# Four heads in lockstep, and TensorE's order written out, in the recurrent part of a diffusion block

## The chip, the core and the metric

The kernel runs on one core of a Trainium2 chip. The metric is the device time of one execution in microseconds; the median of two runs is given for the kernel before. The engines are named as in the profile: PE (TensorE, with PEld for its weight loads), DVE (VectorE), ACT (ScalarE), POOL (GpSimd) and SP, whose queue issues nearly all DMA transfers.

## What is computed

One layer on 512 latent tokens of 1,024 channels, with 256 context tokens ahead of them. A normed and modulated h is multiplied by w_in; the columns feed a Hyena branch, a two-way RWKV-7 branch and 2,048 gates. Both branches are projected, merged under the gates and projected again; a mixture of 16 experts (2,048 wide, 64 tokens each) follows, whose weights are 403 MB. The recurrence is, for each of 8 heads of 64 channels and each direction:

```python
def step(S, inp):
    w_t, k_t, v_t, a_t, b_t = inp[:5]
    sa = einsum('bhij,bhj->bhi', S, a_t)
    S = S * w_t + sa[..., None] * b_t + v_t[..., None] * k_t
    y = einsum('bhij,bhj->bhi', S, inp[5])
    return S, y
# y = groupnorm(y forward + y backward) + bonus, times a gate from a low-rank projection
# gates: sigmoid(h @ w_in[:, gate columns]);  mixed = (g_hy * y_hy + g_rw * (y_rw @ rw_proj)) @ w_out
```

The state starts from a scan over the context. All values are float32.

## The kernel before

The program has stages: modulation, norms and the filter; the Hyena part, which also makes the columns of the recurrent part; the recurrent part; merge, output projection and router; the experts.

The recurrent part is worked in chunks of 64 tokens (`C`), eight of the sequence and four of the context each way. Two heads make a group `g`, since two heads of 64 channels fill the 128 partitions; there are four groups, and each has three batches `bt` of four chunks in both directions. For a batch, `pieces` makes the scaled keys, rates and receptances (`pus` matmuls, a scan on DVE, exponentials on ACT); `scores` makes the masked 64x64 scores `M` of a chunk and writes them to the DRAM tile `N_d`; `inverses` reads them back as 16x16 blocks (`nb`), inverts these on DVE and writes them to `X_d`; `levels` reads those (`XX`) and builds the 64x64 inverses with 32x32 matmuls; `values` transposes values (`pv`) and keys (`pb`). Then `steps` runs the four chunks one after another: `p1` (values and state against scores and keys), a copy to `X1` on DVE, `p2` (the inverse), copies to `UV` on DVE and ACT, `p3` (the new state) and the outputs into the bank `ya`. `epilogue` norms and gates a group's output and stores it to `y_d`.

Work of one group is ahead of or behind that of the next by the strings `ORD0` and `ORD1` and by scheduler priorities (`HP`, `HPB`); the scheduler orders all engines. `gates(i)`, sixteen tiles of 128 gate columns at the end of the program, is what the scheduler puts into TensorE's free time. Each takes a 512 KB tile of w_in from a pool of `NRAW` = 3 buffers and multiplies it by `hraw`, the h that stays in SBUF. `pump` adds matmuls of zeros (`zl`) behind each of `p1`, `p2` and `p3`, and `plv` two behind each step of `levels`:

```python
for _ in range(n):            # pump: into the idle half of the bank bk
    mm(bk[...], zl, zw, start=True, stop=True)
# plv: for i in range(NPL): mm(half, zl, zeros) -- ahead of each level's products
pump(NP1, p1, last)           # steps, behind p1; NP2 behind p2, NP3 behind p3
```

A float32 matmul of at most 512 columns is two records in the trace, so a count of records is twice that of the matmuls. All DMA transfers of the part are issued by SP in the order of its queue; where one has to wait for a buffer, those behind it wait too. After the stage, `halves` (line 1235) loads projection weights through the same raw buffers.

## Time and profile before

| | |
|---|---|
| runs | 1875.36 and 1876.31 us, median 1875.84 |
| profiled execution | span 1886.6 us, the only time given for it |
| recurrent stage | 322 to 782 us |
| merge, output projection, router | 782 to 928 us |
| experts | 928 us to the end |
| busy over the span | PE 90%, PEld 59%, DVE 36%, ACT 23%, POOL 11% |

A row of the table of windows has start and end of a stretch, its length, the busy time of PE, PEld, DVE, ACT and POOL (instructions in brackets), TensorE's granted clock as a share of 2.4 GHz, the mean busy share of the 16 DMA engines and the GB/s they moved. A group by line has line, engine, operation, tiles written and read, shapes and count, then busy time and mean ns of one, then the idle time of the engine just ahead of it and what ended it. The timeline has start and length in us. Tile numbers are left out of the names there.

### The profile page before, as it was taken

How to read it: one execution, taken by the hardware profiler on the slowest of the kernel's cores; microseconds unless marked ns; L12 is line 12 of the kernel's file. 1: busy time of each engine (PE TensorE's matmuls, PEld its weight loads, DVE VectorE, ACT ScalarE, POOL GpSimd, SP SyncE). 2: the span in 40 equal slices, each digit the busy share in tenths (PEclk: the TensorE clock that was granted, in tenths of full speed). 3: DMA queues.
4: the chain of work that ended last, by engine and by line, in shares of the span. 5: the costliest groups of instructions: out<-in, count | busy, mean ns of one | idle time of the engine just before them, and what ended most of it. 6: DMA issues, size and time to landing. Idle time of an engine off the chain costs nothing.

```text
span 1886.6 us, 32798 instructions
## 1 busy us (share of the span) xinstructions
PE 1702.4 (90%) x14006; PEld 1107.5 (59%) x14006; DVE 681.9 (36%) x1520; ACT 434.5 (23%) x941; POOL 214.5 (11%) x255
## 2 busy tenths in 40 slices
PE   8898999999999999789599999889899898998985
PEld 3466786667666767668475545555455454554542
DVE  4765875867584742363500202002020020200203
ACT  3544531434453433333100000000000000000001
POOL 0534102422131300020000000000000000000000
PEclk5799999899999899999699999999999999999998
DMA  7255543433222221571799999999999999999995
GB/s 304 95 187 192 172 159 114 144 83 67 64 69 40 57 47 41 179 269 62 295 402 427 426 427 427 426 427 426 427 427 427 426 427 426 426 426 427 426 427 231
DMA packets 143292, 516.46 MB, mean 274 GB/s; under 512 B 83259, under 2 KB 87499, under 8 KB 118572
## 3 DMA queue, kind: packets, MB, share of 16 engines
q1 hardware_dynamic: 139824, 509.68, 68.8%
q10 hardware_dynamic: 3324, 4.70, 0.7%
q8 instruction: 110, 1.80, 0.4%
q14 instruction: 34, 0.28, 0.0%
HBM read 490.98 MB, written 23.36 MB: 273 GB/s over the span
## 4 chain that ended last, share of the span: by engine, by line
PE 39%; DMA 14%; DVE 3%; ACT 1%; issue 1%; POOL 0%; SPq 0%; DVEq 0%; ACTq 0%; POOLq 0%
PE ph L1425 17%; DMA exp_w<-in_exp_w 12%; PE py L1438 10%; PE px L1392 3%; PE pso L1460 3%; PE pht L249 1%; DVE hd L216 1%; PE po L1245 1%; PE po L1242 1%; PE po L1243 1%; ACT hT L212 1%; PE pl L1326 0%; PE pbq L1406 0%; PE pbp L1402 0%; DMA w_hy_proj<-in_hy_proj 0%
## 5 line engine op out<-in xcount | busy, mean ns | idle before, releaser
L1425 PE MATMUL ph<-exp_w,xe 128*64 128x256 f32 x4096 | 469.2, 380 | 26.7 <-DMA exp_w<-in_exp_w 26.7
L1425 PEld LDWEIGHTS ph<-exp_w,xe 128*64 128x64 f32 x4096 | 318.2, 137 | 194.8 <-issue 63.4
L216 DVE TENSOR_TENSOR hd<-ph,hd 128x256 f32<-128x256 f32 x64 | 27.2, 425 | 674.5 <-PE ph L1425 674.5
L1438 PE MATMUL py<-exp_w,hT 128*64 128x512 f32 x1024 | 236.8, 598 | 24.8 <-ACT hT L212 24.8
L1438 PEld LDWEIGHTS py<-exp_w,hT 128*64 128x64 f32 x1024 | 78.4, 136 | 138.7 <-issue 92.8
L719 PE MATMUL pgate<-hraw,w_gate 128*128 128x256 f32 x512 | 148.0, 409 | 0.7 <-ACT yo L212 0.3
L213 ACT ACTIVATE hd<-ph 128x256 f32<-128x256 f32 x64 | 24.5, 383 | 431.7 <-PE ph L1425 431.7
L719 PEld LDWEIGHTS pgate<-hraw,w_gate 128*128 128x128 f32 x512 | 90.6, 198 | 19.2 <-issue 3.8
L212 ACT ACTIVATE hT<-pht 128x256 f32<-128x256 f32 x64 | 24.5, 383 | 284.6 <-PE pht L249 284.6
L1392 PEld LDWEIGHTS px<-OH,xn 128*128 128x128 f32 x512 | 65.8, 197 | 23.4 <-issue 22.4
L1399 POOL COPY sel<-kcon 16x128 f32<-16x128 f32 x8 | 2.2, 283 | 609.4 <-PE pbq L1406 609.4
L1460 PE MATMUL pso<-ye,oT 128*128 128x512 f32 x128 | 68.7, 628 | 0.7 <-ACT ye L212 0.7
L1392 PE MATMUL px<-OH,xn 128*128 128x128 f32 x512 | 68.0, 282 | 0.9 <-DVE OH L223 0.9
L249 PE MATMUL pht<-kcon,hd 128*128 128x128 f32 x128 | 28.0, 301 | 36.1 <-DVE hd L216 35.9
L216 DVE TENSOR_TENSOR mo<-pso,mo 128x512 f32<-128x512 f32 x56 | 38.4, 691 | 39.3 <-PE pso L1460 39.3
L249 PEld LDWEIGHTS pht<-kcon,hd 128*128 128x128 f32 x128 | 12.9, 141 | 65.2 <-DVE hd L216 65.2
L882 PE MATMUL ps<-ar,bk 64*64 64x64 f32 (+1 forms) x512 | 46.5, 277 | 3.6 <-POOL bk L216 2.0
L882 PEld LDWEIGHTS ps<-ar,bk 64*64 64x64 f32 (+1 forms) x512 | 37.4, 177 | 16.5 <-POOL bk L216 5.0
L1443 DVE COPY ye<-py 64x512 f32<-64x512 f32 x16 | 11.1, 694 | 95.8 <-ACT ye L212 95.8
L216 POOL TENSOR_TENSOR mw<-mw 128x256 f32<-128x256 f32 x32 | 31.5, 1001 | 99.2 <-DVE mw L219 99.2
L288 PE MATMUL p<-zl 128*128 128x256 bf16 x140 | 40.0, 286 | 0.0
L212 ACT ACTIVATE sf<-st,fs 128x64 f32<-128x64 f32 x80 | 24.3, 341 | 49.6 <-DVE st L219 49.4
(396 smaller groups left out, 2549.7 us busy)
## 6 DMA issues: line engine op xcount, KB each, us to landing
exp_w<-in_exp_w SPq DMA_DIRECT2D x192, 2048.0 KB, 31.0
mw<-in_mod_w SPq DMA_DIRECT2D x48, 512.0 KB, 3.9
w_gate<-in_w_in SPq DMA_DIRECT2D x16, 512.0 KB, 4.9
w_h<-in_w_in SPq DMA_DIRECT2D x12, 512.0 KB, 4.1
w_c<-in_w_in SPq DMA_DIRECT2D x12, 512.0 KB, 5.6
g_d<-gt SPq DMA_DIRECT2D x16, 256.0 KB, 4.7
gg<-g_d SPq DMA_DIRECT2D x16, 256.0 KB, 5.5
w_o<-in_w_out SPq DMA_DIRECT2D x8, 512.0 KB, 5.3
```

The costliest lines, as they stand in the source:

```text
L212: return A.activation(out, in_, func, scale=scale, **kw)
L213: return A.activation(out, in_, func, bias=bias, scale=scale, **kw)
L216: e.tensor_tensor(out, a, b, op=op)
L249: TE.transpose(out, in_, ident[0:n, 0:n])
L288: mm(bk[:, 256:256 + NPW].rearrange("p (a b) -> p a b", b=P), zl, zw, start=True, stop=True)
L719: mm(pt[:, n:n + 256], w[:, k, :], hraw[:, k, n:n + 256], start=k == 0, stop=k == KD - 1)
L882: mm(pss[h][r, j * W:(j + 1) * W], BK[d](c)[HR[h], r], AR[d](c)[HR[h], 0:W], start=True, stop=True)
L1242: mm(pt, lhs[0][a], rhs[0][b], start=i == 0, stop=False)
L1392: mm(pt[:, k4 * P:(k4 + 1) * P], xn[:, n, k * P:(k + 1) * P], OH[:, n].rearrange("p a b -> p (a b)"), start=n == 0, stop=n == 3)
L1425: mm(ph[i][64 * hf:64 * hf + 64, 0:256], xe[:, k, 64 * e1:64 * e1 + 64], ws[i][:, k, hf * 256:(hf + 1) * 256], start=k == 0, stop=k == KD - 1)
L1438: mm(py[64 * dh:64 * dh + 64, :], hT_[:, i * P + 64 * hf:i * P + 64 * hf + 64], w2[:, 2 * hf + i, dh * 512:(dh + 1) * 512], start=b == 0 a ...
L1460: mm(pt, oT[:, n * P:(n + 1) * P], ye[:, dh * 512:(dh + 1) * 512], start=True, stop=True)
```

## The change

The recurrent part is written anew. Four heads (two groups, `sg`) go in lockstep, so that there are six units of one batch of two groups, and each matmul block, copy and state update covers four heads. TensorE's order in the stage is written out by `weave`, which runs through the units, the epilogues and the gates as streams with assumed times (`GRP`, `HOP`) and takes the first that is free; the other engines and queues are still ordered by the scheduler. There are no matmuls of zeros in the stage. The scores are made in quarters, 64 rows by 64 columns, and for the chunks of the sequence in two parts. Values are transposed once in the Hyena part, written to `vt_d`, and read back by 48 loads. h is written to `h_d` and read back in four quarters of 128 tokens (`hh`, one buffer); the gates are made for a quarter at a time, so that each 512 KB weight tile is loaded four times: 64 loads, through raw buffers of which there are now two. The decay weights of all groups are loaded at the start through one buffer. Keys (`BK`) have one buffer.

**TensorE, a chunk of the recurrence** (line numbers of the kernel at hand; the numbers in tile names are the program's; `p` is p1, p2 or p3, `zl` the zeros). Before, late in the last group:

```order
L1070 MATMUL p_7802<-st_7793,ar_6564 64x64 x2
L1070 MATMUL p_7802<-st_7797,ar_6601 64x64 x2
L288 LDWEIGHTS zl
L288 MATMUL p_7802<-zl 128x256
L719 MATMUL pgate_8188<-hraw,w_gate_8186 128x256 x2
L1076 MATMUL p_7813<-X_7801,xf_2382 64x64 x4
L288 LDWEIGHTS zl
L288 MATMUL p_7813<-zl 128x256
L719 MATMUL pgate_8188<-hraw,w_gate_8186 128x256
L1085 MATMUL p_7821<-UV_7500,BT_7502 64x64
```

Now, in the fourth unit:

```order
L1044 MATMUL p_6019<-st_5997,AR_4499 64x64 x8
L688 MATMUL pgate_6040<-hh_5428,w_gate_6041 128x128 x8
L1050 MATMUL p_6051<-X_6018,xf_2442 64x64 x8
L688 MATMUL pgate_6040<-hh_5428,w_gate_6062 128x128 x8
L1058 MATMUL p_6072<-UV_5407,BT_5408 64x64 x8
...
L1075 MATMUL yb_6084<-AR_4499,st_5997 64x64 x8
```

Each block has eight matmuls in place of four (rows that repeat for p1's first half and the outputs are left out between the last two), the zeros are gone, and a whole gate tile, eight 128-column matmuls, stands in a hop.

**SP, around the first inverses.** Before, in the first group of the stage:

```order
L715 DMA w_gate_7966<-in_w_in 128x1024
L889 DMA N_d_2372<-M_2460 64x8x64
L889 DMA N_d_2372<-M_2461 64x8x64
L903 DMA nb_2504<-N_d_2372 64x16x16
L715 DMA w_gate_7988<-in_w_in 128x1024
...
L715 DMA w_gate_8010<-in_w_in 128x1024
L930 DMA X_d_2374<-rb_2505 64x16x16
L931 DMA X_d_2374<-rt_2506 64x16x16
...
L964 DMA X_2722<-X_d_2374 32x16x32 x4
```

Now, in the first unit (`hh` is h read back, `N_d`, `nb`, `X_d` and `X` the way of scores and inverses through DRAM):

```order
L686 DMA w_gate_2891<-in_w_in 128x1024
L891 DMA nb_2804<-N_d_2433 128x16x16
L1158 DMA hh_2888<-h_d 128x1024
L693 DMA g_d<-gt_2885 128x4x128
L686 DMA w_gate_2907<-in_w_in 128x1024
L686 DMA w_gate_2932<-in_w_in 128x1024
L918 DMA X_d_2435<-rb_2805 128x16x16
L919 DMA X_d_2435<-rt_2806 128x16x16
L686 DMA w_gate_2942<-in_w_in 128x1024
L939 DMA X_3032<-X_d_2435 32x16x32
L686 DMA w_gate_2963<-in_w_in 128x1024
L939 DMA X_3032<-X_d_2435 32x16x32
```

Gate weights stand between all legs of the inverses' way; 23 of their loads are ahead of the last loads of `X`, where six were.

**TensorE, the end of the stage.** Before:

```order
L1097 MATMUL ya_7547<-ar_6601,st_7839 64x64 x2
L719 MATMUL pgate_8210<-hraw,w_gate_8208 128x256 x2
L1120 MATMUL pmu_7873<-y_7871,kcon 128x512
L719 MATMUL pgate_8210<-hraw,w_gate_8208 128x256 x4
L1127 MATMUL pva_7878<-kcon,sq_7876 128x2 x4
L719 MATMUL pgate_8210<-hraw,w_gate_8208 128x256 x6
L1136 MATMUL pvb_7888<-kcon,vw_7886 128x128 x4
L1141 MATMUL pg_7896<-sg,gup_5994 128x512
L719 MATMUL pgate_8232<-hraw,w_gate_8230 128x256 x16
```

Now:

```order
L1044 MATMUL p_7852<-st_7830,AR_6513 64x64 x8
L1050 MATMUL p_7870<-X_7851,xf_2442 64x64 x8
...
L1075 MATMUL yb_7881<-AR_6513,st_7830 64x64 x8
L1096 MATMUL pmu_7901<-Y_2474,kcon 128x512
L1104 MATMUL pva_7906<-kcon,sq_7904 128x2 x4
L1114 MATMUL pvb_7916<-kcon,vw_7914 128x128 x4
L1120 MATMUL pg_7924<-sg,gup_7899 128x512
L1096 MATMUL pmu_7930<-Y_2474,kcon 128x512
L1104 MATMUL pva_7935<-kcon,sq_7933 128x2 x4
L1114 MATMUL pvb_7945<-kcon,vw_7943 128x128 x4
L1120 MATMUL pg_7953<-sg,gup_7928 128x512
L1215 MATMUL ppr_8029<-yh_7991,wh_hy_proj 128x512
```

The gates no longer lie beside the last epilogue; they end 426 rows ahead of it, and two epilogues follow one another.

The core of the diff:

```diff
-HP = 2000
-HPB = 300
-ORD0 = 'P0ail1b^2ucxjvw'
-ORD1 = "P0aiXuy'l12x^bcjY^ZvwE"
-NP1, NP2, NP3, NPW = 1, 1, 1, 256
...
-NRAW = 3
+NRAW = 2
...
+GRP, HOP = 0.65, 1.45
+NMS, NAR, NBK, NUV, NBT = (3, 2), 3, 1, 2, 2
...
-                ts(V, hraw[:, k, :], ph, modA[:, 0, k, 0:1], mcol[:, 0, k, 0:1], ALU.mult, ALU.add)
-                tt((V, G)[HB[k]], hT[1][:, k, :], hraw[:, k, :], hT[0][:, k, :], ALU.subtract)
+                hraw = ep.tile([P, T], F32, tag="hraw", bufs=3, name=f"hraw{k}")
+                ts(V, hraw, ph, modA[:, 0, k, 0:1], mcol[:, 0, k, 0:1], ALU.mult, ALU.add)
+                tt((V, G)[HB[k]], hT[1][:, k, :], hraw, hT[0][:, k, :], ALU.subtract)
+                SY.dma_start(out=h_d[:, :, k].rearrange("h p t -> p h t"), in_=hraw.rearrange("p (h t) -> p h t", h=4))
...
+                        vt = hp.tile([P, 6, P], F32, tag="vt", name=f"vt{m}")
+                        for a, b in ((0, 4), (4, 6)):
+                            pv = pxx(f"pv{m}{a}")
+                            for i in range(a, b):
+                                transpose(pv[:, (i - a) * P:(i - a + 1) * P], cz[:, i * P:(i + 1) * P])
+                            act(vt[:, a:b].rearrange("p n c -> p (n c)"), pv[:, 0:(b - a) * P], AF.Copy)
+                        SY.dma_start(out=vt_d[m - 8].rearrange("(n p) c -> p n c", p=P), in_=vt)
...
-        def gates(i):
-            o = HY + RW + (i % 2) * D + (i // 2) * P
-            w = filler[0](f"w_gate{i}").rearrange("p (k f) -> p k f", k=KD)
-            SY.dma_start(out=w, in_=w_in[o // P])
-            pt = pfl(f"pgate{i}")
-            for n in (0, 256):
+        def gates(i, q, h):
+            pt = pfl(f"pgate{q}{i}")
+            for n in range(4):
+                o = HY + RW + ((i + n) % 2) * D + ((i + n) // 2) * P
+                w = raw_tile(f"w_gate{q}{i + n}").rearrange("p (k f) -> p k f", k=KD)
+                SY.dma_start(out=w, in_=w_in[o // P])
                 for k in range(KD):
-                    mm(pt[:, n:n + 256], w[:, k, :], hraw[:, k, n:n + 256], start=k == 0, stop=k == KD - 1)
-            t_ = fp.tile([P, T], F32, tag="stg", bufs=NST, name=f"gt{i}")
+                    mm(pt[:, P * n:P * n + P], w[:, k, :], h[:, k, :], start=k == 0, stop=k == KD - 1)
+                    if k % 4 == 3:
+                        yield 0.9, 0.0
+            t_ = fp.tile([P, T], F32, tag="stg", bufs=NST, name=f"gt{q}{i}")
             act(t_, pt, AF.Tanh, scale=0.5)
-            SY.dma_start(out=g_d[i], in_=t_)
+            SY.dma_start(out=g_d[i:i + 4, :, q * P:q * P + P].rearrange("n p t -> p n t"),
+                         in_=t_.rearrange("p (n t) -> p n t", n=4))
...
+            def weave(streams):
+                at, wait, todo = [0.0] * len(streams), [None] * len(streams), list(range(len(streams)))
+                while todo:
+                    free = [i for i in todo if wait[i] is None or wait[i]()]
+                    i = next((i for i in free if at[i] <= clock[0]), None)
+                    if i is None:
+                        clock[0] = min(at[i] for i in free)
+                        continue
+                    wait[i] = None
+                    r = next(streams[i], False)
+                    if r is False:
+                        todo.remove(i)
+                    elif callable(r):
+                        wait[i] = r
+                    else:
+                        clock[0] += r[0]
+                        at[i] = clock[0] + r[1]
...
+                        for j in range(4):
+                            o = C * (4 * d + j)
+                            for r in HR:
+                                for h in range(2):
+                                    bk = BK[HR[h], gi, d, at(d, j)].rearrange("p a t -> p (a t)")
+                                    mm(pss[h][r, o:o + C], bk[:, r], AR[HR[h], gi, d, at(d, j), cols_], start=True, stop=True)
...
                     p1 = bank("st", 2, f"p1{nm}{j}")
-                    for d in range(2):
-                        c = cs[d][j]
-                        o = d * C
-                        for h in range(2):
-                            last = mm(p1[HR[h], o:o + C], M[h][:, d, j, 0:C], uv[:, d, ju, 64 * h:64 * h + 64], start=d == 0,
-                                      stop=first and d == 1)
+                    for gi, d, h in quad:
+                        mm(four(p1)[HR[h], gi, d], M[h][:, gi, d, j], UV[:, gi, d, j, 64 * h:64 * h + 64],
+                           start=gi == 0 and d == 0, stop=first and gi == 1 and d == 1)
+                    yield GRP, max(0.0, t_st - clock[0] - GRP)
                     if not first:
-                        for d in range(2):
-                            c = cs[d][j]
-                            o = d * C
-                            for h in range(2):
-                                last = mm(p1[HR[h], o:o + C], AR[d](c)[HR[h], 0:C], st[d][HR[h]], start=False, stop=d == 1)
-                    pump(NP1, p1, last)
-                    V.tensor_copy(X1.rearrange("p d i -> p (d i)"), p1[:, 0:2 * C])
+                        for gi, d, h in quad:
+                            mm(four(p1)[HR[h], gi, d], AR[HR[h], gi, d, lc[d], 0:C], st[HR[h], gi, d], start=False,
+                               stop=gi == 1 and d == 1)
+                    V.tensor_copy(X1, four(p1))
+                    yield GRP, HOP
                     p2 = bank("st", 2, f"p2{nm}{j}")
-                    for d in range(2):
-                        for h in range(2):
-                            last = mm(p2[HR[h], d * C:(d + 1) * C], X[d][HR[h], j], X1[HR[h], d], start=True, stop=True)
-                    pump(NP2, p2, last)
-                    p23 = p2[:, 0:2 * C].rearrange("p (d i) -> p d i", d=2)
-                    V.tensor_copy(uv[0:64, :, ju, 0:64], p23[0:64])
-                    act(uv[64:128, :, ju, 64:128], p23[64:128], AF.Copy)
-                    if n < NCH - 1:
+                    for gi, d, h in quad:
+                        mm(four(p2)[HR[h], gi, d], X[HR[h], gi, d, j], X1[HR[h], gi, d], start=True, stop=True)
+                    V.tensor_copy(UV[0:64, :, :, j, 0:64], four(p2)[0:64])
+                    act(UV[64:128, :, :, j, 64:128], four(p2)[64:128], AF.Copy)
+                    yield GRP, HOP
+                    old = st
+                    if bt < 2 or j < 3:
                         p3 = bank("st", 2, f"p3{nm}{j}")
-                        for d in range(2):
-                            for h in range(2):
-                                last = mm(p3[HR[h], d * C:(d + 1) * C], btt[:, d, jh, 64 * h:64 * h + 64],
-                                          uv[:, d, ju, 64 * h:64 * h + 64], start=True, stop=True)
-                        pump(NP3, p3, last)
+                        for gi, d, h in quad:
+                            mm(four(p3)[HR[h], gi, d], BT[:, gi, d, j, 64 * h:64 * h + 64], UV[:, gi, d, j, 64 * h:64 * h + 64],
+                               start=True, stop=True)
+                        st = new_state(j)
+                        if first:
+                            tt(V, flat4(st), flat4(four(p3)), by4(F[:, j]), ALU.mult)
+                        else:
+                            tt(V, st, four(p3), old, ALU.add)
+                            tt(V, flat4(st), flat4(st), by4(F[:, j]), ALU.mult)
+                        t_st = clock[0] + GRP + HOP + 0.4
+                        yield GRP, 0.0
                     if bt:
...
-            run(ORD0, (0, False))
-            for g in range(4):
-                pair[0], pair[1] = pair[1], None
-                run(ORD1, (g + 1, g == 3))
-            for i in range(16):
-                gates(i)
+            units = [dict(sg=n % 2, bt=n // 2, nm=f"{n % 2}{n // 2}", N_d=N_d[n % 2], X_d=X_d[n % 2], xf=xfs[n % 2]) for n in range(6)]
+            def unit(n):
+                u = units[n]
+                yield lambda: n < 3 or n - 3 in done
+                yield lambda: n < 1 or n - 1 in filled
+                yield from pieces(u)
+                yield 0.0, 10.0
+                yield from scores(u, 0)
+                inverses(u)
+                t_inv = clock[0] + 22.0
+                yield lambda: n < 2 or n - 2 in done
+                if u["bt"]:
+                    yield from scores(u, 1)
+                yield from values(u)
+                filled.add(n)
+                yield lambda: n < 1 or n - 1 in levelled
+                yield 0.0, max(0.0, t_inv - clock[0])
+                yield from levels(u)
+                levelled.add(n)
+                yield from steps(u)
+                done.add(n)
+            def endings(sg):
+                yield lambda: 4 + sg in done
+                for g in (2 * sg, 2 * sg + 1):
+                    yield from epilogue(g)
+            def all_gates():
+                for q in range(4):
+                    hh = fp.tile([P, KD, T // 4], F32, tag="hh", name=f"hh{q}")
+                    SY.dma_start(out=hh, in_=h_d[q])
+                    for i in range(0, 16, 4):
+                        yield from gates(i, q, hh)
+            with tc.manual_schedule(engines={mybir.EngineType.PE}):
+                weave([unit(n) for n in range(6)] + [endings(0), endings(1), all_gates()])
```

## Rows read from the trace of the kernel before

**Rows 1.** Table of windows: stretch, length, busy us (x instructions), clock, DMA share, GB/s.

```profile
322.00:782.00 460.00, 444.13 (x6292) 316.69 (x6290) 264.26 (x772) 189.75 (x489) 104.57 (x152) 0.96 0.30 73
893.00:940.00 47.00, 25.21 (x138) 21.43 (x137) 26.21 (x72) 6.49 (x13) 0.99 (x3) 0.67 0.79 320
928.00:1886.00 958.00, 855.77 (x5921) 497.86 (x5920) 129.81 (x291) 71.70 (x167) 8.74 (x9) 0.99 0.97 411
```

**Rows 2.** Groups by line, TensorE, 300 to 800 us: count, busy, mean ns.

```profile
L719 PE MATMUL pgate<-hraw,w_gate 128*128 128x256 f32 x512 | 148.0, 409 | 0.7 <-ACT yo L212 0.3 <-ACT gt L213 0.3
L882 PE MATMUL ps<-ar,bk 64*64 64x64 f32 (+1 forms) x512 | 46.5, 277 | 3.6 <-POOL bk L216 2.0 <-DVE rb L915 1.1 <-DVE M L216 0.5
L288 PE MATMUL p<-zl 128*128 128x256 bf16 x140 | 40.0, 286 | 0.0
L1063 PE MATMUL p<-UV,M 128*64 128x64 f32 x384 | 27.6, 239 | 0.4 <-ACT UV L212 0.2
...
L941 PE MATMUL lvs<-zl 128*128 128x256 bf16 x120 | 24.2, 284 | 2.2 <-DVE X L216 1.4 <-DVE PP L216 0.5
...
L1076 PE MATMUL p<-X,xf 64*64 64x64 f32 x384 | 22.2, 232 | 0.2 <-DVE rb L915 0.2
```

**Rows 3.** Timeline, 750 to 756 us: start, length, engine, line, operation, tiles, count.

```profile
749.97 0.45 PE L1063 MATMUL p<-UV,M 128*64 128x64 f32 x8
750.35 0.31 PEld L1070 LDWEIGHTS p<-st,ar 64*64 64x64 f32 x8
750.36 0.45 PE L1070 MATMUL p<-st,ar 64*64 64x64 f32 x8
...
755.31 0.45 PE L1070 MATMUL p<-st,ar 64*64 64x64 f32 x8
```

**Rows 4.** First line of the page.

```profile
span 1886.6 us, 32798 instructions
```

**Rows 5.** Timeline at the stage's start, the first levels and later levels.

```profile
324.47 2.19 POOL L216 TENSOR_TENSOR us<-ur,us 64x256 fp32r<-64x256 f32 x2
...
333.90 0.69 PE L882 MATMUL ps<-ar,bk 64*64 64x64 f32 x32
...
391.34 0.24 PE L973 MATMUL lvs<-X,M 32*32 32x32 f32 x2
...
718.38 0.38 PE L941 MATMUL lvs<-zl 128*128 128x256 bf16 x2
...
726.83 0.30 DVE L1008 COPY xf<-lvs 32x128 f32<-32x128 f32 x1 [0.33 <-ACT xf L212]
```

**Rows 6.** Timeline at the end of the recurrent part and the merge's start.

```profile
764.22 0.60 ACT L212 ACTIVATE y<-ya 128x512 f32<-128x512 f32 x1 [1.34 <-PE ya L1097]
...
771.14 1.05 PE L1136 MATMUL pvb<-kcon,vw 128*128 128x128 f32 x8
...
775.66 0.32 SPq L1143 DMA_DIRECT2D y_d<-y  x1
...
782.23 0.33 SPq L1235 DMA_DIRECT2D w_hy_proj<-in_hy_proj  x1
...
789.91 0.80 PE L1242 MATMUL ppr<-yh,wh_hy_proj 128*128 128x512 f32 x1 [8.90 <-DMA w_hy_proj<-in_hy_proj]
```

**Rows 7.** DMA issues, 322 to 800 us: count, KB, median us to landing.

```profile
w_gate<-in_w_in SPq DMA_DIRECT2D x15, 512.0 KB, 4.9
...
X<-X_d SPq DMA_DIRECT2D x48, 64.0 KB, 2.5
...
ur<-in_ups ACTq DMA_DIRECT2D x3, 256.0 KB, 3.7
...
nb<-N_d SPq DMA_DIRECT2D x4, 128.0 KB, 3.0
```

**Rows 8.** Groups by line, DVE, the recurrent stage.

```profile
L816 DVE TENSOR_TENSOR_SCAN gs<-kcon,w 128x256 f32<-128x256 f32 x24 | 20.8, 866 | 0.2
```

586 lines of the change are left out of this document (251 added, 335 removed).

## The prediction

> **What bounds the kernel now.** I read the table of windows first. The expert stage, from 928 us to the end, keeps the DMA engines 0.97 busy at 411 GB/s [rows 1]: it streams the expert weights and can only start earlier, so a microsecond won ahead of it is a microsecond of the kernel. In the recurrent stage (322 to 782 us) TensorE is busy 444.13 of 460 us at a granted clock of 0.96, DVE 264, ACT 190, and the DMA engines 0.30 [rows 1]: the amount of work on TensorE sets its length. The groups by line say what this work is [rows 2]: 148.0 us of gate projections, 46.5 of scores, 40.0 and 24.2 of zeros, and six groups of 64x64 step matmuls (the first, 27.6, and the last, 22.2, are shown; together 149.5). The timeline of the last chunks [rows 3] shows the other limit, the chain: the second half of p1 starts at 750.36 and that of the next chunk at 755.31; that is 4.95 us for a chunk of two heads, and gates and zeros fill its holes.
>
> The sum is made on the profiled execution, whose span is 1886.6 us [rows 4] and for which no other time is given; the median of the runs is 1875.84, 10.8 less. I apply the difference to the median.
>
> **Work on TensorE.**
> - *Zeros.* 140 + 120 matmuls go, 64.2 us [rows 2].
> - *Scores.* 1,280 records, all in the quartered form: 32 of them took 0.69 us [rows 5], so 28 us in place of 46.5.
> - *Steps.* 125 blocks of 16 records. A block of 8 needs 0.31 us of weight loading, and p1's second half starts 0.39 us after its first [rows 3]; I take 0.65 us for 16, between 0.62 and 0.78, so 81 us in place of 149.5.
> - *Gates.* 1,024 records of 128 columns. Eight such records took 1.05 us [rows 6], 0.13 each, the start of the first included; without it I take 0.11, so 113 us (134 at most) in place of 148.0.
> - *The rest* (levels, transposes, projections, epilogues), counted from the order at the rates of like rows, comes to about 80.
>
> That is some 300 us in place of 444, so 144 could go. Less goes, since work must still lie where the holes are.
>
> **The stage on its new path**, in times of the profile.
> 1. *Start.* The values are now transposed in the hyena part (24 transposes and their copies), h goes out to DRAM in eight writes that stand on SP ahead of the first hyena weights, and raw weights have two buffers instead of three. The nearest prices are 24 x 0.13 = 3 us [rows 6] and eight issues of 0.32 on SP [rows 6]. I take +8 us, with 3 and 15 as ends: the stage begins at 330.
> 2. *To the first levels.* Before, they began at 391.34 [rows 5]. Two paths now lead to them. On the one, four decay weights come one after another through one buffer, each 3.7 us of transfer [rows 7] and 2.19 us of subtraction [rows 5], and the pieces need that buffer, so they follow 24 us after the start. Then come the pieces of two groups (about 20 us: four scans of 0.87 [rows 8] with some six shorter DVE operations behind each), the scores, and the inverses, whose way through DRAM has four transfers of 2.5 to 3.0 us [rows 7] and, with the DVE work between, takes about 22. On the other path, 21 gate tiles stand ahead of the levels in TensorE's order and 23 of their loads in SP's. A tile's load lands in 4.9 us [rows 7]; with two buffers, 1.8 us of matmuls and 0.35 of issue, one tile is done each 3.5 us, and 21 need 75 us. Both paths end at about 405.
> 3. *To the last gate.* 181 us of work by the rates above, and 11 us where neither a hop's end nor a gate is ready: 597. The other 43 tiles have 192 us, 4.5 each against the 3.5 that they need, but they come in bunches (the last four in 11 us of work), h is read back four times into one buffer, and SP's queue is in order: behind a load that waits for a buffer stand the score writes and inverse reads, and behind these the next load. I add 15 us (0 to 35): 612. The 25 MB more of gate weights are no load on bandwidth: 73 GB/s flow here now, 411 in the expert stage [rows 1].
> 4. *The tail.* From there TensorE has about 66 us of work and no filler. A chain orders it: the last batch's pieces 20, scores 8, inverses 22, levels 10 (a batch of two heads took 8.6, from 718.38 to 727 [rows 5]), four chunks of 6 us (4.95, blocks and copies twice as wide), two epilogues 20 (one took 11.4, from its y at 764.22 to the store at 775.66 [rows 6]): 104. Work with holes lowers the clock: in 893 to 940 us TensorE was busy 25.2 of 47 us, and the granted clock was 0.67 [rows 1], a mix of its levels of 1.2 and 2.4 GHz. I add 15 us (5 to 35), since only part of the chain is TensorE's: 731 for the last store of y, against 775.66, so 45 earlier. The Trainium skill (TensorE: Matmul & The Clock Gate, HAM oscillation) says that an engine that idles between bursts falls back to half rate again and again, which speaks against taking the zeros out. By that page alone the 66 us would double, and the time would be about 1886.
> 5. *The merge.* Before, the first projection weights were issued at 782.23, behind the last gate, and the merge's first matmul ran at 789.91, 14.3 us after y's store [rows 6]. The gates are now long done, and I take 10 us: 4 won. Two buffers for its 21 raw tiles cost 8 (0 to 15). Net +4.
>
> DVE and ACT I cost at nothing: both do the same elements in fewer, wider instructions, and TensorE's work covers them until 612. Without that cover they lengthen the hops of the tail, where I have counted them.
>
> The sum: 45 - 4 = 41 us earlier, **1835 us**.
>
> **Rivals.**
> - *All covered* (0.20). The allowances in 1 to 4 (8 + 11 + 15 + 15) and the 4 of the merge vanish: 94 us earlier, 1782. DVE, ACT and the DMA engines have room for it [rows 1]; against it speaks that the order was written for assumed hops and knows nothing of loads.
> - *The clock falls in the whole stage* (0.11). Without zeros the stage gets some 0.85, the tail 0.67 as in the row above [rows 1]: 181 / 0.85 is 32 more and 66 / 0.67 is 33 more, less the 15 already taken: 1885. Against it: until 612 gates stand in nearly every hop.
> - *The gate weights set the pace: slower* (0.17, half of it slower by over 2%). 64 loads of 512 KB replace 16, through two buffers instead of three. TensorE's order is fixed, so a late tile stops all four heads. With both buffers in flight a tile costs 3.5 us; with one, because the next load is queued behind a write that waits for DVE, 4.9 + 1.8 + 0.35 = 7.1 us [rows 7]. At 5.0 us a tile the gates, begun at 330, end at 650 and the kernel takes 1873; from there on nothing is won; past 5.6 it is slower by over 2%; at 6.2, three tiles in four alone, 1950. For it: such writes stand between the loads of every batch. Against: the mean demand is only 4.4 us.
> - *Preparation sets the pace* (0.10). Keys have one buffer, so a batch's pieces wait for the transposes of the batch before. I count some 45 us a batch; at 60 the sixth is ready 75 us later, about 40 of them beside gates: 1870.
>
> My forecast has 0.42. A measurement of this kernel can tell about 2% from no change, so faster means under 1838.3 and slower over 1913.4. The forecast's own range, 1805 to 1860, has 0.25 of its chance below 1838; with the first rival and 0.05 for mild forms of the others that makes 0.50 faster; 0.39 within; 0.11 slower, nearly all of it late weights. To hold the time 8 times in 10 the range goes from 1778, the covered case, to 1895, past the clock and mildly late weights.
>
> **What would show it.** In the profile after: TensorE busy some 300 us from the hyena part's end to the last store of y, and no zeros there (over 330, and the rates are wrong); first levels near 405, last gate near 612; in the table of waits, TensorE's waits ahead of gates put down to the transfer of w_gate, 15 to 60 us in sum (over 100 speaks for late weights); a granted clock over 0.9 until the last gate and about 0.8 behind it; about 119 us from the last gate to the last store; an expert stage of 958 us as before. The forecast is wrong if the gates end after 650, or if the tail takes over 150 us.

## The result, and the profile after

The kernel is slower: 2027.62 us (2024.38 to 2030.86) against 1875.84, a ratio of 1.0809 (95% interval 1.0734 to 1.0884). The profiled execution has a span of 2022.5 us against 1886.6 [rows 4], 135.9 more, and the account below is made on the spans. The medians lie 151.8 us apart; the 15.9 more are not placed by it.

In this section a stage runs from the end of the hyena part (its last matmul, 345.30 us; 322.50 before) to the last store of y. The table of windows of the kernel after, columns as in [rows 1]; its stretches, in order, are start to first levels, to the last gate, to the last store, the whole stage, merge up to the first matmul of the experts, and the experts:

```profile
345.30:461.00 115.70, 73.12 (x538) 63.84 (x536) 28.84 (x59) 25.85 (x57) 22.03 (x31) 0.78 0.62 170
461.00:762.70 301.70, 224.06 (x4717) 195.20 (x4717) 129.98 (x294) 74.16 (x186) 50.54 (x70) 0.82 0.53 136
762.70:910.60 147.90, 93.69 (x2006) 69.43 (x2005) 60.08 (x128) 30.15 (x72) 22.51 (x26) 0.69 0.18 39
345.30:910.60 565.30, 390.87 (x7258) 328.47 (x7256) 218.89 (x480) 130.16 (x315) 95.08 (x127) 0.78 0.46 118
910.60:1075.20 164.60, 120.80 (x558) 97.33 (x558) 83.92 (x151) 44.32 (x71) 14.84 (x12) 0.83 0.61 222
1064.00:2022.00 958.00, 855.72 (x5922) 497.68 (x5921) 129.74 (x291) 71.82 (x167) 8.77 (x9) 0.99 0.97 411
```

The same stage before:

```profile
322.50:775.70 453.20, 438.32 (x6266) 311.90 (x6265) 262.35 (x769) 188.26 (x487) 104.57 (x152) 0.96 0.29 71
```

The hyena part ends 22.8 us later, the stage is 112.1 longer, the merge 1.0 (it took 163.6 before); the experts are the 958 us at 411 GB/s that they were [rows 1]. The stage is longer with *less* on TensorE: 390.87 us busy in place of 438.32, and 174 us idle in place of 15. The granted clock fell from 0.96 to 0.78.

The groups by line on TensorE in the stage, columns as in [rows 2]:

```profile
L688 PE MATMUL pgate<-hh,w_gate 128*128 128x128 f32 x1024 | 163.0, 318 | 42.6 <-DMA w_gate<-in_w_in 32.1 <-DMA hh<-h_d 8.4 <-ACT gt L176 1.4
L870 PE MATMUL ps<-AR,BK 64*64 64x64 f32 x1280 | 25.8, 222 | 4.3 <-DVE M L179 2.4 <-issue 1.9
...
L1050 PE MATMUL p<-X,xf 64*64 64x64 f32 x384 | 19.1, 247 | 5.4 <-DVE X L1046 5.4
...
L1039 PE MATMUL p<-UV,M 128*64 128x64 f32 x384 | 17.8, 241 | 0.0
...
L849 PE MATMUL pbs<-bs,kcon 128*128 128x512 f32 x8 | 8.2, 1125 | 45.4 <-DVE bs L179 45.4
```

The records are those that were counted, and there are no zeros, but the busy time is 390.87 us where I had 300. Scores are 25.8 (28 in the forecast), gates 163.0 (113, at most 134), and a `pbs` record takes 1,125 ns. Part of the stage runs at the low level of the clock (1.2 GHz); in the wait from 770.70 to 782.76 us, just ahead of a `pbs`, the granted clock is 0.50. 390.87 x 0.78 is 305, a rough scaling, near the work that was forecast. The product of `pbs` before, where its tile is called `pus`, took little over half as long and TensorE hardly waited ahead of it:

```profile
L862 PE MATMUL pus<-bs,kcon 128*128 128x512 f32 x8 | 4.4, 628 | 0.4 <-DVE bs L216 0.4
```

What is new is the idle time at the right, and the table of TensorE's waits in the stage (waiting line and what ended the wait: us in total, times, longest) sums it by cause:

```profile
PE pbs L849 <- DVE bs L179: 45.4, 4, 13.4
PE pgate L688 <- DMA w_gate<-in_w_in: 32.1, 20, 4.4
PE pus L793 <- ACT w L176: 31.4, 24, 10.1
PE pus L793 <- DMA UV<-vt_d: 9.3, 1, 9.3
PE pgate L688 <- DMA hh<-h_d: 8.4, 2, 4.5
```

No one wait is large enough for 174 us. What they have in common shows when one follows the six units instead. Each unit's `inverses` begins with one read of `nb`, so the row of these reads is a clock of the preparation (minimum, median and maximum duration, then start of the first and of the last). The kernel after, then the one before:

```profile
L891 SPq DMA_DIRECT2D nb<-N_d x6: 377/380/383, 426.0 to 829.0; - x6
```

```profile
L903 SPq DMA_DIRECT2D nb<-N_d x8: 371/592/603, 346.7 to 666.3; - x8
```

Six reads in 403.0 us are one each 80.6 us (the five gaps are 71.8, 64.8, 79.5, 99.1 and 87.8; the waits on `bs` lie in the last two). Before, eight reads came 45.7 us apart, beside the steps of the group ahead; each group has two there, one for its first batch and one for the other two, so that the same work, twelve batches of one group, took 319.6 us from the first read to the last. The stage after is therefore 80.7 us to the first read, 5 x 80.6, and 81.6 from the last read to the last store.

The timeline of TensorE while the last unit is prepared (the gates are over, the levels of the fifth unit are in hand):

```profile
768.77 1.93 PE L949 MATMUL lv<-X,M 32*32 32x32 f32 x128
...
782.79 2.04 PE L849 MATMUL pbs<-bs,kcon 128*128 128x512 f32 x2 [12.09 <-DVE bs L179]
...
788.29 1.08 PE L949 MATMUL lv<-PP,X 32*32 32x32 f32 x64
...
794.45 1.08 PE L949 MATMUL lv<-X,M 32*32 32x32 f32 x64
...
808.91 2.05 PE L849 MATMUL pbs<-bs,kcon 128*128 128x512 f32 x2 [13.38 <-DVE bs L179]
```

TensorE's order stands, so two `pbs` products that wait 12 and 13 us for `bs` hold the levels of the fifth unit behind them, though these are another unit's work. Ahead of the first of the two the timeline of the other engines has

```profile
779.33 2.59 POOL L179 TENSOR_TENSOR kr<-k,rz 64x512 f32<-64x512 f32 x2
...
781.95 0.69 DVE L179 TENSOR_TENSOR bs<-bs,kr 128x512 f32<-128x512 f32 x1 [3.98 <-POOL kr L179]
...
782.56 0.68 DVE L179 TENSOR_TENSOR PP<-lv,kcon 128x512 f32<-128x512 f32 x1
```

The wait is a chain that goes back and forth between three engines (from 770.70 to 782.76 us DVE is busy 3.78 us, ACT 3.97, POOL 6.58). And DVE holds the fifth unit too: `PP`, the next step of its levels, has its input at 770.70 and is made behind `bs`, in the order that the scheduler gave DVE. From the first `pus` of the last unit's pieces (762.75) to its scores at 820.23 pass 57 us. The steps then run as foreseen (last unit, second product of its first two chunks; those of the other two follow at 882.25 and 887.37, each 5.12 us apart):

```profile
872.01 0.68 PE L1050 MATMUL p<-X,xf 64*64 64x64 f32 x16 [0.62 <-DVE X L1046]
...
877.13 0.68 PE L1050 MATMUL p<-X,xf 64*64 64x64 f32 x16 [0.53 <-DVE X L1046]
```

### The profile page after: what moved, and what is told of

Same layout as the page of the kernel before. It is cut to its first block, busy times and chain, and to the rows that moved or that the text cites. A ratio compares the mean times of both kernels' runs of the same rounds, so it can differ in the third digit from the quotient of the medians.

```text
span 2022.5 us, 34384 instructions
## 1 busy us (share of the span) xinstructions
PE 1661.5 (82%) x14998; PEld 1127.1 (56%) x14998; DVE 633.1 (31%) x1232; ACT 379.0 (19%) x777; POOL 202.3 (10%) x230
## 4 chain that ended last, share of the span: by engine, by line
PE 41%; DMA 14%; DVE 5%; issue 2%; ACT 2%; POOL 1%; SPq 0%; DVEq 0%; ACTq 0%; POOLq 0%
PE ph L1398 16%; DMA exp_w<-in_exp_w 11%; PE py L1411 9%; PE px L1365 3%; PE pso L1433 3%; PE pht L212 1%; DVE hd L179 1%; PE pgate L688 1%; PE po L1218 1%; PE po L1215 1%; PE po L1216 1%; ACT hT L175 1%; PE lv L949 1%; PE pl L1299 0%; PE pbq L1379 0%
## 5 line engine op out<-in xcount | busy, mean ns | idle before, releaser
L688 PE MATMUL pgate<-hh,w_gate 128*128 128x128 f32 x1024 | 163.0, 318 | 42.6 <-DMA w_gate<-in_w_in 32.1
L688 PEld LDWEIGHTS pgate<-hh,w_gate 128*128 128x128 f32 x1024 | 146.4, 225 | 53.6 <-DMA w_gate<-in_w_in 26.8
L1411 PEld LDWEIGHTS py<-exp_w,hT 128*64 128x64 f32 x1024 | 78.1, 136 | 138.8 <-issue 93.0
L1433 PE MATMUL pso<-ye,oT 128*128 128x512 f32 x128 | 68.7, 628 | 0.7 <-ACT ye L175 0.7
L793 PE MATMUL pus<-lh,us 128*128 128x256 f32 x48 | 22.3, 464 | 43.0 <-ACT w L176 31.4
L849 PE MATMUL pbs<-bs,kcon 128*128 128x512 f32 x8 | 8.2, 1125 | 45.4 <-DVE bs L179 45.4
L793 PEld LDWEIGHTS pus<-lh,us 128*128 128x128 f32 x48 | 11.2, 234 | 53.0 <-ACT w L176 24.5
L179 DVE TENSOR_TENSOR M<-ps,kcon 128x256 f32<-128x256 f32 x80 | 29.2, 416 | 33.8 <-PE ps L870 33.8
```

The source lines that it names most:

```text
L179: e.tensor_tensor(out, a, b, op=op)
L688: mm(pt[:, P * n:P * n + P], w[:, k, :], h[:, k, :], start=k == 0, stop=k == KD - 1)
L793: mm(pu, us[g][:, i, d, :], lh[:, i, sl], start=True, stop=False)
L1411: mm(py[64 * dh:64 * dh + 64, :], hT_[:, i * P + 64 * hf:i * P + 64 * hf + 64], w2[:, 2 * hf + i, dh * 512:(dh + 1) * 512], start=b == 0 a ...
L1433: mm(pt, oT[:, n * P:(n + 1) * P], ye[:, dh * 512:(dh + 1) * 512], start=True, stop=True)
```

## The experiments

An experiment computes all that its base does unless its expectation says what it leaves out. Ratios are to runs of the kernel before made beside it.

**Was it the amount of work?** The first group changes the work on TensorE and leaves the rest.

*e4: the kernel before without zeros.*
```diff
-NP1 = 1; NP2 = 1; NP3 = 1; NPL = 2
+NP1 = 0; NP2 = 0; NP3 = 0; NPL = 0
```


> The kernel before, without its 260 matmuls of zeros in the recurrent part (the one that opens the output bank stays). Theory B: the clock of the stage falls from 0.96 to 0.9 or below, and the kernel loses 10 to 30 us. Theories A and C: gates fill the hops as before, TensorE has 64 us less to do, the clock stays above 0.93, and the kernel gains 10 to 40 us.

1873.33 us, ratio 0.9974 (0.9935 to 1.0014). Its stage:

```profile
313.90:766.10 452.20, 419.60 (x6029) 302.45 (x6027) 259.06 (x769) 188.42 (x487) 105.88 (x152) 0.92 0.29 72
```

The zeros are gone, 18.7 us of busy time with them, the clock is 0.92 in place of 0.96, and the stage is 452.2 us in place of 453.2. The 64.2 us of [rows 2] lay in holes and bought no time that can be measured.

*e7: the kernel before with one product of eight of each gate; e14: the same with eight zeros for one behind each step.*
```diff
-for k in range(KD): mm(pt[:, n:n+256], w[:, k, :], hraw[:, k, n:n+256], ...)
+mm(pt[:, n:n+256], w[:, 0, :], hraw[:, 0, n:n+256], start=True, stop=True)
-NP1 = 1; NP2 = 1; NP3 = 1        # e14 only
+NP1 = 8; NP2 = 8; NP3 = 8
```


> The kernel before with one of the eight products of each gate column (wrong gates): some 130 us of TensorE's 444 leave the stage. Theory P, on which the forecast rests (work on TensorE sets the stage's length): the stage falls from 453 us by 80 us or more. Theory D' (a chain sets it already in the kernel before, and gates and zeros only fill its holes): by under 30 us.

> The kernel before with one of the eight products of each gate column (wrong gates), as in e7, but with eight matmuls of zeros for one behind each of p1, p2 and p3: about as much work as the gates had, in the same holes. Theory B (a low clock lengthens the chain): the stage's clock is back at 0.93 or more, and the stage back from 504 us to 450 to 465. Theory D' alone (a chain that the clock does not touch): the stage stays over 490.

e7 took 1906.83 and 1935.94 us, too far apart for a ratio; the shorter is still 31 us above the kernel before. Its profile is of the longer one, so its stage shows what can happen and is no measure of the loss. e14 took 1990.33, ratio 1.0575 (1.0391 to 1.0758). The two stages, e7 first:

```profile
321.80:826.20 504.40, 446.54 (x5841) 308.54 (x5839) 264.54 (x769) 186.62 (x485) 102.70 (x152) 0.68 0.26 64
```

```profile
314.10:872.80 558.70, 493.99 (x6821) 353.18 (x6819) 268.73 (x769) 186.06 (x485) 103.42 (x152) 0.87 0.24 58
```

The gates take 28.8 us in place of 148.0 [rows 2], 119 less, and the kernel became longer, not shorter. With little filler its clock is 0.68 in this execution, and the same steps and scores take longer at it. In e14 the clock is back at 0.87 and the stage is 558.7 us. That does not clear the clock: eight zeros take 1.05 us (e14, from 611.84), all of the 1.0 us that passed before from the end of p1 to p2 (606.3 to 607.4), so that anything else put into the hop lengthens it (to 1.4 us there). How much of the 558.7 us this explains, no run shows. e4 and e7 answer the question all the same: the kernel before did not get faster when work left its stage.

*e2: the kernel after with zeros (one behind each product of a step, 30 ahead of each `pbs`).*
```diff
+zeros(p1)                        # and p2, p3
+for _ in range(30): zeros(pb)    # ahead of pbs
```


> One matmul of zeros goes back behind each of p1, p2 and p3, and 30 ahead of each pbs, where TensorE waits 8 to 13 us anyway; nothing else changes. Theory B (the low clock, 0.82 in the gate phase and 0.69 in the tail, is what costs): the clock of the tail rises to 0.85 or more and the kernel gains 20 to 40 us. Theories A and C: the clock may rise, but the waits stay, so the gain is under 12 us, or a loss of up to 10 us from 70 more matmuls.

2019.56 us, against 2027.62 after; ratio 1.0750 (1.0697 to 1.0803). The stage:

```profile
341.40:903.80 562.40, 420.01 (x7448) 347.15 (x7446) 220.64 (x480) 130.25 (x315) 95.17 (x127) 0.82 0.45 118
```

Busy time rises by 29 us and the clock to 0.82 (in the tail from 0.69 to 0.76), the wait for `bs` falls from 45.4 to 24.5, and the stage is 562.4 us in place of 565.3. The Trainium skill (TensorE: Matmul & The Clock Gate, HAM oscillation) says that idling between bursts re-throttles the engine; the rows agree on the clock, but the zeros that raised it gave back next to nothing here.

**Was it the written order?**

*e1: `pbs` 12 us later in the order.*
```diff
 tt(V, bs[g], bs[g], kr, ALU.mult)
+yield 0.0, 12.0
 pb = pmm(f"pbs{g}")
```


> Theory A (TensorE's written order makes it stand behind chains): the bonus matmul pbs stands directly behind pus in the order and TensorE waits 45.4 us ahead of it, in four waits of 8 to 13 us, with levels and steps of the other unit queued behind. Here the order puts other streams' work for 12 us between the two. A expects these waits to fall under 10 us and the kernel to gain 25 to 45 us (1980 to 2000). Theory B (the clock): TensorE's holes only move, no gain of over 10 us. Theory C (late gate weights, in-order SP): no gain either, since the gates set the pace until 762 us; at most the 25 us of the two waits behind the last gate.

2020.56 us, ratio 1.0756 (1.0703 to 1.0809); stage 562.9. The largest wait of the table is gone, and others stand in its place (waits of TensorE in the stage):

```profile
PE pgate L688 <- DMA w_gate<-in_w_in: 36.2, 24, 5.2
...
PE lv L950 <- DMA X<-X_d: 27.1, 12, 10.9
```

The second was 6.1 us in the kernel after. A wait that is taken off the top of the table is no gain while the unit behind it is no sooner: the reads of `nb` are 80.2 us apart.

*e3: TensorE's order left to the scheduler.*
```diff
-with tc.manual_schedule(engines={mybir.EngineType.PE}):
+if True:
     weave([unit(n) for n in range(6)] + [endings(0), endings(1), all_gates()])
```


> The program is the same, but TensorE is ordered by the scheduler like the other engines, not by the written order. Theory A: the waits ahead of pbs, pus and gates (118 us in all) fall by more than half, and the kernel gains 50 to 100 us. Theory C: gate weights stay late (64 loads, two buffers), so the gain is under 20 us. Theory B: no gain, since no work is added that fills holes.

1949.86 us, ratio 1.0379 (1.0323 to 1.0436). Busy time as after (386.63), stage 490.6, and the reads of `nb`:

```profile
L891 SPq DMA_DIRECT2D nb<-N_d x6: 376/380/929, 404.8 to 748.4; - x6
```

68.7 us apart in place of 80.6. 75 of the 112 us by which the stage had grown come back by the order alone, with the same instructions. Of these 75 us, 70 are idle time of TensorE (174 to 104 us) and 4 its busy time, while the clock rose from 0.78 to 0.85: what the order cost was waiting.

*e9: the written order with hops nearer to those measured (36 us for an inverse in place of 22; 8 behind `pus`; 12 ahead of `pbs`).*
```diff
-t_inv = clock[0] + 22.0
+t_inv = clock[0] + 36.0
+yield 0.0, 8.0                   # behind pus
+yield 0.0, 12.0                  # ahead of pbs
-yield 0.0, 10.0                  # between pieces and scores
+yield 0.0, 8.0
```


> The written order keeps its rules but gets times measured in the changed kernel: 36 us from scores to levels (was 22), 8 us behind the decay projections of a group of pieces (was 2), 12 us ahead of pbs (was 0). Theory A (the written order stands in the wrong places because its assumed times are too short): the waits ahead of pbs, pus and levels fall by 60 us, and the kernel gains 40 to 80 us, as much as with the scheduler's order (77). Theory D (the chain of preparation is the bound whatever the order): it gains under 20 us.

2063.8 us, ratio 1.0923 (1.0756 to 1.1089), 36 us more than after: worse. The first levels come 168.6 us behind the start, in place of 115.7. The stretches from there to the last gate and on to the last store:

```profile
509.00:642.80 133.80, 106.92 (x2224) 94.42 (x2224) 55.09 (x130) 30.71 (x74) 14.72 (x25) 0.94 0.61 165
642.80:946.10 303.30, 199.19 (x4259) 154.39 (x4257) 131.43 (x286) 68.02 (x170) 53.48 (x68) 0.65 0.22 48
```

Told that hops are long, the planner fills them with gates and runs out of gates at 642.80; 303 us without filler follow, at 0.65. So longer hops alone do not mend the order; that better times could, under other rules, is not excluded.

**Was it the preparation, one unit behind the other?**

*e8: two key buffers; a unit's pieces may begin once those of the unit ahead are done.*
```diff
-NMS, NAR, NBK, NUV, NBT = (3, 2), 3, 1, 2, 2
+NMS, NAR, NBK, NUV, NBT = (2, 2), 3, 2, 2, 2
-yield lambda: n < 1 or n - 1 in filled
+yield lambda: n < 1 or n - 1 in pieced
+yield lambda: n < 2 or n - 2 in done      # ahead of scores
```


> The changed kernel with two buffers for the keys, and a unit's pieces allowed in the order as soon as the unit before has its pieces (not its transposes); the masked scores get two buffers for three to make room. Theory D: the scores come 8 to 20 us sooner from unit to unit, and the kernel gains 30 to 80 us. Theory A (the fixed order's waits): TensorE gets more waits ahead of pus, gain under 20. Theory C: none.

The masked scores have two buffers for three here, and for that a unit's scores wait in the order for the steps of the unit two ahead (last line of the diff). The same goes for e10, e12, e13, e15 and e16.

1987.31 us, ratio 1.0584 (1.0483 to 1.0685); stage 521.4. The reads of `nb`:

```profile
L891 SPq DMA_DIRECT2D nb<-N_d x6: 370/382/478, 424.8 to 754.0; - x6
```

65.8 us apart, 74 sooner in all; 45 of these are won at the second unit (27.0 us behind the first, 71.8 after), and the other four gaps are still 75.5 on average. But the stage gains 44: from the last read to the last store it is now 114.5 us in place of 81.6. The inverses of the last unit take as long as after (24 us), but gate tiles, which end only at 885.2, behind the last store (868.5), stand between its levels (26 us from the first to the first step, 17 after) and in the hops of its chunks (p2 at 808.5, 816.0, 827.6 and 835.3 us, 7.5 to 11.6 apart in place of 5.12).

**Was it the gate weights?**

*e5: the kernel after with one product of eight of each gate, all loads kept; e6: 16 loads in place of 64, all products kept; e10: three raw buffers (and two of masked scores, with the rule of e8).*
```diff
-for k in range(KD): mm(pt[:, P*n:P*n+P], w[:, k, :], h[:, k, :], ...)   # e5
+mm(pt[:, P*n:P*n+P], w[:, 0, :], h[:, 0, :], start=True, stop=True)
+if n == 0:                                                             # e6
     w = raw_tile(...); SY.dma_start(out=w, in_=w_in[o // P])
-NRAW = 2                                                               # e10
+NRAW = 3
```


> The changed kernel with one of the eight products of each gate column (the gates are wrong by that; every weight load stays): some 100 us of TensorE's work leave the stage. Theory D, formed after the first four runs (the units' preparation, one after another, is the bound: scores come every 63 to 99 us, and inverses take 32 to 48 us, not 22): the stage, now 565 us, shrinks by under 60 us. Theory P (TensorE's work sets the length, as forecast): by 100 us or more.

> The changed kernel with 16 gate weight loads in place of 64 (three tiles of four multiply by the first tile's weights, so the gates are wrong by that; TensorE's work is unchanged). Theory C (late weights and an in-order SP queue): the 40 us of waits ahead of gates and part of the slow inverse round trips go, and the kernel gains 50 us or more. Theory D: round trips get 5 to 10 us shorter for each of the first units, the gain is 15 to 50 us, and the tail stays near 148.

> Three raw weight buffers in place of two, and room for them from two buffers of masked scores for three. All 64 loads stay. Theory C in its buffer form: waits ahead of gates fall from 40 to under 15 us, the Hyena part ends 5 to 15 us sooner, and the kernel gains 30 to 55 us, as with 16 loads (48). Theory C in its queue form (64 loads stand in SP's order ahead of the score writes and inverse reads, whatever the buffers): it gains under 20 us.

e5: 2071.58 us, ratio 1.1033 (1.0960 to 1.1106), stage 606.5. Cheap gates are all put first, and TensorE waits for their weights (waits in the stage):

```profile
PE pgate L687 <- DMA w_gate<-in_w_in: 98.1, 54, 4.8
```

The issues of these loads:

```profile
L686 SPq DMA_DIRECT2D w_gate<-in_w_in x64: 327/328/1187, 302.0 to 528.5; - x64
```

Two of them are issued at 302.0, ahead of the stage, and the other 62 from 358.1 to 528.5, one each 2.79 us. Behind them, with no gates at all, the units still come 66.4 us apart (first read 539.0, last 871.0), at a clock of 0.65. So the gates' work is not what spaces the units in the main: without it the spacing is 14 us less, and what the lower clock adds to the 66.4 is open. e6: 1969.06 us, ratio 1.0487 (1.0395 to 1.0579), stage 514.3, units 73.6 apart. e10: 1977.79, ratio 1.0468 (1.0304 to 1.0632), stage 525.1, units 75.2 apart; its waits on w_gate are 4.2 us in place of 32.1, and its hyena part ends at 334.2. Late weights thus cost 40 to 50 us of the stage, 14 to 21 of it ahead of the first levels (these come after 94.8 us in e6 and 101.9 in e10, in place of 115.7). The third buffer shows in the hyena part as well: the nine versions of the kernel after with two end it between 340.4 and 347.1 us, the three that have three buffers and the transposes (e10, e12, e13) between 333.7 and 336.5.

*e11: the kernel before with two raw buffers.*
```diff
-NRAW = 3
+NRAW = 2
```


> The kernel before with two raw weight buffers for three. If the 19 to 23 us by which the Hyena part ends later in the changed kernel come from the buffers, it ends at 330 us or later (322.5 in the profile of before, 314 without zeros), and the kernel loses 8 to 25 us; if they come from the transposes, copies and writes that were put there, it stays within 5 us.

1890.85 us, ratio 1.0047 (1.0006 to 1.0087); hyena end at 310.0, stage 450.4. The buffer that costs 40 us of the stage after costs the kernel before half a per cent, and does not delay its hyena part.

**Together.**

*e16: e3 and e8.* 

> The changed kernel with TensorE's order left to the scheduler (as e3, stage 490.6 us) and two key buffers (as e8, stage 521.4 us against 565.3), gates and loads as in the changed kernel. If the written order and the single key buffer are two separate causes, their gains add: 75 + 44, stage 440 to 455 us, kernel 1900 to 1920. If both only take out the same waiting of preparation (the scheduler already runs the pieces of the next group early), the stage stays near e3's: 480 to 495 us, kernel 1940 to 1955. If late gate weights are what is left, the waits on w_gate and hh grow past 30 us.

1939.62 us, ratio 1.0323 (1.0256 to 1.0389); stage 466.8. Reads of `nb`:

```profile
L891 SPq DMA_DIRECT2D nb<-N_d x6: 365/380/473, 408.7 to 697.2; - x6
```

57.7 us apart, the shortest of all, and the stage lies between the first two expectations: 24 us below e3's, where e8 alone gave 44. The order and the key buffer are in part the same waiting. The kernel gains only 10 us on e3, because the gates now end at 827.6, 20 us behind the last store at 807.9: what is late next is the filler.

*e12: the scheduler's order, three raw buffers (and two of masked scores, with the rule of e8), h in halves (32 gate loads, 256 columns a product).*
```diff
-h_d = tc.dram_tile([4, P, KD, T // 4], F32, ...)
+h_d = tc.dram_tile([2, P, KD, T // 2], F32, ...)
```


> Scheduler order for TensorE, three raw buffers, and h read back in halves of 256 tokens, so that gate weights are loaded 32 times for 64 and the gates have half as many, wider matmuls. If the gains of the scheduler's order (77 us) and of fewer loads (48) add up, 1890 to 1915 us; if both remove the same waits, 1935 to 1950.

1910.7 us, ratio 1.0113 (0.9957 to 1.0268), within the expectation that the gains add, and the best of the versions with four heads that leave nothing out. From the kernel before it can't be told. Its stretches as above, and its reads of `nb`:

```profile
336.50:422.70 86.20, 76.92 (x476) 58.64 (x474) 34.79 (x70) 30.23 (x68) 24.80 (x35) 0.86 0.61 170
422.70:658.00 235.30, 209.23 (x4268) 160.67 (x4267) 124.28 (x284) 69.58 (x175) 46.82 (x65) 0.88 0.49 121
658.00:796.80 138.80, 93.48 (x2006) 70.14 (x2004) 59.65 (x128) 29.81 (x72) 22.84 (x28) 0.75 0.19 42
336.50:796.80 460.30, 379.63 (x6746) 289.45 (x6744) 218.72 (x480) 129.62 (x315) 94.46 (x127) 0.84 0.42 106
```

```profile
L891 SPq DMA_DIRECT2D nb<-N_d x6: 376/383/692, 393.9 to 715.3; - x6
```

Units 64.3 us apart, stage 460.3: nearly that of before, with the tail still 138.8 us at 0.75. Against the profile of before its span is 23.6 us longer: 14.0 by the later end of the hyena part (336.5), 7.1 in the stage, 2.5 in the merge.

*e15: e12 without the 24 value transposes and their copies.*
```diff
-for a, b in ((0, 4), (4, 6)): ...   # transposes of cz into vt
-SY.dma_start(out=vt_d[...], in_=vt)
+SY.dma_start(out=vt_d[...], in_=cz.rearrange("p (n c) -> p n c", c=P))
```


> As e12, without the 24 transposes of the values and their eight copies in the Hyena part (untransposed values are stored in their place, so the output is wrong). If these delay the Hyena part, it ends at 326 us or sooner (336.5 in e12); if it is the writes of h or the buffers, at 333 or later.

Hyena end at 324.3 in place of 336.5, stage 461.9; 1902.31 us, ratio 1.0107 (0.9958 to 1.0256). The transposes and copies that I priced at 3 us of TensorE cost 12 of the path in the profile, and 8 by the medians.

*e13: e12 with the writes of h on ACT's queue and another buffer for `ur`.*
```diff
-ur = rq.tile(..., tag="gs"); SY.dma_start(out=h_d[...])
+ur = rq.tile(..., tag="rz"); A.dma_start(out=h_d[...])
```


> As e12, and the decay weights go through the buffer of rz in place of that of gs, and the eight writes of h are issued by ACT's queue in place of SP's. If the decay weights hold up the first pieces, the first levels come 8 to 15 us sooner after the Hyena part's end (86 us in e12); if the writes of h hold up SP, the Hyena part ends 8 us sooner or more (336.5 in e12). Both: 1890; neither: 1905 to 1915.

1913.99 us, ratio 1.0169 (1.0018 to 1.0321). To the first levels:

```profile
333.70:410.10 76.40, 66.68 (x400) 50.58 (x398) 29.36 (x60) 26.34 (x58) 22.41 (x31) 0.89 0.65 182
```

The first levels come after 76.4 us in place of e12's 86.2, and the stage is 460.7 in place of 460.3. An early start is lost again among the units: their reads take 327.1 us in place of 321.4.

No version with four heads is shown to be faster than the kernel before; e12 and e15, whose intervals reach below 1, and e13 (1.0018 at least) are within 2% of it by their medians.

## Why the prediction was wrong

The forecast was 1835 us and the range 1778 to 1895; the kernel took 2027.62. **The step that failed is the first:** "the amount of work on TensorE sets its length", and with it step 3, which made the way to the last gate from 181 us of work and small allowances. The 0.97 busy share of [rows 1] was made of a chain and of filler in its holes. e4 takes filler out and nothing happens; e7 takes 119 us of it out and the kernel is no faster (1906.83 us at best); after, 47 us less busy time stand in a stage 112 us longer. The Trainium skill (Perfetto Trace Analysis, Identifying the Most-Contended Engine) warns that matmul busy share is not a good measure of how near TensorE is to its limit; the rows agree for another reason than the one it gives: there it is that matmuls are pipelined, here that gates and zeros ran where nothing else could.

Set against the forecast by the reads of `nb`, my steps put the first read 53 us behind the start (75 less 22 for the inverses), the last at 640 (612 + 20 + 8), and the last store 91 behind that:

| | forecast | after | e3 | e8 | e12 | e16 |
|---|---|---|---|---|---|---|
| start to first read | 53 | 80.7 | 63.8 | 77.7 | 57.4 | 67.6 |
| five units | 257 | 403.0 | 343.6 | 329.2 | 321.4 | 288.5 |
| last read to last store | 91 | 81.6 | 83.2 | 114.5 | 81.5 | 110.7 |
| stage | 401 | 565.3 | 490.6 | 521.4 | 460.3 | 466.8 |

Of the 164 us by which the stage was missed, 146 are the spacing of the units. That is the mechanism of the fourth rival, preparation, which I gave 0.10 and priced at 60 us a batch; it is 80.6. I had counted a batch as work (45 us) and not as a string of hops, each of which stands in one order with gates, steps and levels of other units. For the last unit its parts can be read: the pieces take 57 us and the scores 9. The experiments give three causes for the spacing, which overlap: the written order (e3, 12 us a unit), one key buffer (e8, 15 us), and the gate weights through two buffers (e10, 5 us), the third rival's mechanism. That rival's mark, over 100 us of waits on w_gate, was not met (32.1 us), but e10 gives 40 us of stage back; that the order spreads a late tile over all streams is a likely reason, and not shown. With the order and the key buffer both mended (e16) 57.7 us a unit are left, where my steps come to 51.4; what sets these was not tested.

By steps:
1. *Start.* +8 forecast, +22.8 measured. About 12 are the transposes (e15), priced by their records alone, and about 8 the second raw buffer (e10, e12 and e13 against the nine with two), so that both terms were named and too small. These are rough: the kernel before itself ended its hyena part between 310.0 (e11) and 322.5 (its own profile, whose span is 10.8 us above the median of its runs).
2. *To the first levels.* 75 forecast, 115.7 measured. Both paths were named. The weights' path was the longer by up to 21 us (94.8 with 16 loads, e6), and the other one too is longer than the 75. In e13, with the decay weights (which ACT's queue loads, [rows 7]) in another buffer, the levels come 10 us sooner than in e12.
3. *To the last gate.* 207 from the first levels forecast, 301.7 measured: 224.06 busy at a clock of 0.82 (forecast over 0.9) in place of 181, and 78 idle in place of 26. 224.06 x 0.82 is 184, so by this rough scaling the work was sized right, and the clock and the waits were not. That the gates ended after 650 was the mark of a wrong forecast.
4. *Tail.* 119 forecast, 147.9 measured. The pieces took 57 in place of 20, the inverses 23 (22), the levels 17 in place of 10, with two epilogues of the other groups between; the chunks 5.12 each in place of 6, the last two epilogues 20 as forecast. The clock was 0.69, near the 0.67 that I had read [rows 1].
5. *Merge.* Net +4 forecast, +1.0 measured, but neither term is there: the first matmul comes 17.0 us behind y's store (927.6) and not 10, so nothing was won, and with three raw buffers the merge takes 166.3 us (e10) against 164.6, so the 8 do not show. That the sum is near is luck. The experts' 958 us held.

To cost DVE and ACT at nothing was wrong in kind: it holds only while TensorE's work covers them, and nothing covered the 12 us of their chain with POOL ahead of `pbs`.

Open is how much of the stage is the clock. Less filler lowers it (0.78 after, 0.68 in e7's profile) and products at 1.2 GHz are longer, but e2's higher clock gave 3 us, and e14 raised it by zeros that stood in the chain. Not tried were two key buffers in e12, the pieces with their chain moved to other engines, and four heads in lockstep with h and the weights as they were before, so that what lockstep by itself is worth stays open too.

## What to carry to other kernels

A high busy share is a bound only if the work in it is work that others wait for: take the filler out of the kernel at hand first, and see whether the time falls. Running chains in lockstep halves the chain of steps (5.12 us a chunk for four heads, 4.95 for two before) but leaves the preparation of each unit in series, so count its hops, not its work, and find one event per unit whose spacing can be read from the trace. A written order on one engine can hold one stream behind the late hop of another, as `pbs` held the levels; it has to be at least as good as the scheduler's at what the scheduler sees, the late transfers included.

## What the runs showed of the hardware that was not expected

- 512 KB loads through two buffers came one each 2.79 us (e5, 62 issued from 358.1 to 528.5 us), where one lands in 4.9 [rows 7].
- Zeros moved the granted clock and hardly the time: 0.78 to 0.82 for 3 us (e2), 0.96 to 0.92 for none (e4).
- The same 128x512 product took 1,125 ns a record in the kernel after (`pbs`, behind waits of 8 to 13 us, with 0.50 granted in the one looked at), 646 (median) in e1, where other work stands ahead of it, and 628 before (`pus`, L862): nearly the whole factor between the two levels of the clock.
